# HGRN2 score products: two decay levels in one unbroken TensorE group, with a copy of the queries for the first level of a pair

## The chip, the core and the metric

The kernel runs on one core of a Trainium2 chip. The metric is the device time of one execution in microseconds (us), lower is better. TensorE is called PE below (its weight loads PEld), VectorE DVE, ScalarE ACT, GpSimd POOL, and SP is the engine that issues most DMAs.

## What is computed

One block of a diffusion transformer on 2048 tokens of width 1024 with 256 context tokens: a mixer of four HGRN2 heads and four retention heads, both run forwards and backwards, an output projection, and a gated convolutional FFN of width 2816. The change is in the HGRN2 heads. Their recurrence has a decay per token and per channel, so the scores of a chunk are not a plain product of queries and keys:

```python
def step(s, inp):
    qc, kc, vc, lfc = inp
    b = jnp.cumsum(lfc, axis=2)
    diff = b[:, :, :, None, :] - b[:, :, None, :, :]
    decay = jnp.where(mask[:, :, None], jnp.exp(jnp.minimum(diff, 0.0)), 0.0)
    attn = jnp.einsum('bhtsk,bhsk->bhts', qc[:, :, :, None, :] * decay, kc)
    o = (jnp.einsum('bhtk,bhkv->bhtv', qc * jnp.exp(b), s)
         + jnp.einsum('bhts,bhsv->bhtv', attn, vc))
```

`q`, `k` and the decay `f` are 128 channels wide; `v` has 128 columns. The score of tokens t and s needs the product of all decays between them.

## The kernel before

The program has three parts: a prologue (modulation vectors, the first norm, the first weights), the eight mixer heads, and the output projection with the FFN. The dense products run in float16 with three products per pair of blocks (`mm3`, lines 98 to 103) on blocks combined in a seven-product scheme.

A head is worked in four steps of 512 tokens, so the HGRN2 heads have 16 steps. A step has two threads of code, which `weave` (line 1003) deals out alternately: the sweep of this step (`hg_sweep1`, line 871) and the projections of the next one (`hg_proj`, line 843, mostly float16 products named `pa`, `pb`, `pc`, `p`). A scheduler then puts each engine's instructions into one fixed order by what is ready and by priority, which is the order in which the code was written unless a piece is marked as urgent. On the chip every engine works through its own fixed order and waits at an instruction whose inputs are not there.

`hg_sweep1` computes the scores of a chunk of 128 tokens by levels 1, 2, 4, ..., 64. At level `lv` a block of `2*lv` tokens is cut into halves; keys `K` and queries `Q` carry the decay up to the border between the halves, for both directions at once. After each level DVE multiplies half of `K` and of `Q` by the decay of the other half (lines 906 and 911), which extends them to the next level. So the products of a level must have read `K` and `Q` before these two multiplications, and the next level's products come after them.

- The diagonal (`sd`, line 881) and the levels 1 to 16 (`sc`, line 895) each take 16 float32 products of 32 by 32 outputs, one for each block of 32 tokens; level 32 (`sf`, line 902) takes 16 of that size and level 64 takes 8 of 64 by 64. A float32 product shows as two passes in the trace, so a level of 16 products is 32 records of PE. They use 32 (or 64) columns of the array, one column group after another.
- For levels 1 to 16 ACT first copies the wanted halves of `K` into a packed tile `Kl` (line 891); `Q` is read where it lies, with a stride.
- The result of a level lies in one of two PSUM buffers with the tag `sc`. DVE merges it into the tile `Ad` under a mask (line 913); the diagonal goes to `Ad` by a copy on ACT (line 882); levels 32 and 64 are copied by ACT into the full score tile `A` (lines 916 and 919).
- Then come transposes of `K` (`kp`), state increments (`uf`, `ub`) and the output products (`op`), all of them float32 products of 128 columns.

ACT and DVE also move the results of the projections out of PSUM (for example `ct` by line 604, `V` by line 644, `FG` by line 782), from three PSUM buffers with the tag `pj`. ACT squares and splits the weights of the next head as well, which arrive by DMA as `raw` (line 742).

Of the kernel before, what the change touches and what calls it, by code (L numbers as in the profile page):

```python
# [9 lines left out]
F32 = mybir.dt.float32  # L10
# [8 lines left out]
P = 128  # L19
# [3 lines left out]
G = 512  # L23
# [6 lines left out]
NIN = 4608  # L30
EPS = 1e-6
WR = 2
KL = 3
B = 32
LEVELS = (1, 2, 4, 8, 16, 32, 64)

V_N1, V_N2, V_LB, V_HN, V_RN, V_BM = 0, 8, 16, 32, 36, 40
NV = 88
KEPT = ("K0", "K1", "Q0", "Q1", "FG", "KTt", "ou0")
BANKS = dict(pj=3, sc=2, tu=3)  # L40
BUFS = dict(z=14, vg=7, q=4, wr=2, xs=3, Kl=KL, A=2, gate=NG + 1)
H = G // 2
# [8 lines left out]
def view(t, off, dims):  # L51
    return bass.AP(t.tensor, t.offset + off, [t.ap[0]] + dims)


class Kern:
# [90 lines left out]
    def setup(self):  # L146
# [37 lines left out]
        mp = self.mp  # L184
        sc = mp.tile([2 * KT, P], F32, tag="Kl", bufs=KL, name="s_c")
        q = nc.gpsimd
# [4 lines left out]
        self.mod_loads()  # L191
        s2 = mp.tile([NV, P], F32, tag="Kl", bufs=KL, name="s2")
        for v, n, src in ((V_BM, 48, I["b_mod"].rearrange("o (a p) -> (o a) p", p=P)),
# [5 lines left out]
            q.dma_start(s2[v:v + n], src)  # L199
        s1 = mp.tile([4 * NF, P], F32, tag="Kl", bufs=KL, name="s1")  # L200
        q.dma_start(s1[:3 * NF], I["conv_w"].rearrange("o j (a p) -> (o j a) p", p=P))
# [13 lines left out]
    def small_vectors(self):  # L215
# [8 lines left out]

        mf = self.mp.tile([P, 5 * B], F32, tag="Kl", bufs=KL, name="mf")
        nc.gpsimd.dma_start(mf, self.I["masks"])
# [22 lines left out]
    def mod_rows(self, rows, nr, j4):  # L249
# [3 lines left out]
        if nr == 2:  # L253
            rs = self.mp.tile([P, 512], F32, tag="Kl", bufs=KL, name="modrow")
            if j4:
# [538 lines left out]
    def hg_context(self, pool, h, W, st):  # L794
# [10 lines left out]
        yield from self.single(*self.tm(w, self.hc, P), dq, lambda half: V[:, half:half + 1])  # L805
        Tc = pool.tile([P, 2, 2], F32, tag="T128", bufs=2, name="cT128")
        o = 2 * n
        for lv in LEVELS:
            nb = n // (2 * lv)
# [61 lines left out]
    def hg_sweep1(self, pool, h, g, slot, pr, st):  # L871

        nc = self.nc
        FG, K, Q, qs, ks, V, gate = (pr[n] for n in ("FG", "K", "Q", "qs", "ks", "V", "gate"))

        A = pool.tile([P, 4, P], F32, tag="A", bufs=2, name="A")
        Ad = pool.tile([P, 4, B], F32, tag="Ad", bufs=1, name="Ad")
        blocks = [(c, slice(j, j + B), c * P + j) for c in range(4) for j in range(0, P, B)]
        sc = self.ps("sc", [P, 4, B], "sd")
        for c, js, o in blocks:  # L880
            nc.tensor.matmul(sc[js, c], ks[:, o:o + B], qs[:, o:o + B], start=True, stop=True, skip_group_check=True)
        nc.scalar.copy(Ad, sc)
        yield
        T = FG
        T128 = pool.tile([P, 2, 4], F32, tag=f"T128_{slot}", bufs=1, name="T128")
        for li, lv in enumerate(LEVELS):
            nb = G // (2 * lv)
            near = 2 * lv <= B
            if near:
                Kl = pool.tile([P, G], F32, tag="Kl", bufs=KL, name="Kl")  # L890
                nc.scalar.copy(Kl.rearrange("p (b two i) -> p b two i", two=2, i=lv), view(K, 0, [[2 * lv, nb], [G + lv, 2], [1, lv]]))
                sc = self.ps("sc", [P, 4, B], "sc")
                for c, js, o in blocks:
                    qv = view(Q, o, [[2 * lv, B // (2 * lv)], [G + lv, 2], [1, lv]])
                    nc.tensor.matmul(sc[js, c], Kl[:, o:o + B], qv, start=True, stop=True, skip_group_check=True)
            else:

                sc = self.ps("sc", [P, 4, lv], "sf")
                for c in range(4):
                    for j in range(P // lv):  # L900
                        o, q = c * P + j * lv, c * P + (j ^ 1) * lv
                        nc.tensor.matmul(sc[j * lv:(j + 1) * lv, c], K[:, j % 2, o:o + lv], Q[:, 1 - j % 2, q:q + lv],
                                         start=True, stop=True, skip_group_check=True)

            kv = view(K, 0, [[G + lv, 2], [2 * lv, nb], [1, lv]])
            nc.vector.tensor_tensor(kv, kv, view(T, 1, [[G // lv - 1, 2], [2, nb], [0, lv]]), ALU.mult)
            Tl = T
            T = self.totals(T, T128 if lv == 64 else
                            pool.tile([P, 2, nb], F32, tag="Ta" if lv in (1, 4, 16) else "Tb", bufs=1, name="T2"))
            qv = view(Q, 0, [[G + lv, 2], [2 * lv, nb], [1, lv]])  # L910
            nc.vector.tensor_tensor(qv, qv, view(Tl, G // lv + 1, [[-G // lv - 1, 2], [2, nb], [0, lv]]), ALU.mult)
            if near:
                nc.vector.copy_predicated(Ad, view(self.masks, li * B, [[0, 4], [1, B]]), sc)
            else:
                for j in range(P // lv):
                    nc.scalar.copy(A[j * lv:(j + 1) * lv, :, (j ^ 1) * lv:((j ^ 1) + 1) * lv], sc[j * lv:(j + 1) * lv])
                if lv == B:
                    for _, js, o in blocks[:P // B]:
                        nc.scalar.copy(A[js, :, o:o + B], Ad[js])
            yield  # L920

        KTt = self.slot_tile([P, 2, 4, P], F32, "KTt", "KTt")
        for d in range(2):
            kp = self.ps("tu", [P, 4, P], "kp")
            for c in range(4):
                nc.tensor.transpose(kp[:, c], K[:, d, c * P:(c + 1) * P], self.ident)
            nc.scalar.copy(KTt[:, d], kp)
        yield
        uf = self.ps("tu", [P, 4, P], "uf")
        for c in range(4):  # L930
            nc.tensor.matmul(uf[:, c], KTt[:, 0, c], V[:, c], start=True, stop=True, skip_group_check=True)
        ou, qf = self.slot_tiles(slot)
        Uf = ou[:, 1].rearrange("p (c t) -> p c t", t=P)
        nc.scalar.copy(Uf, uf)
        nc.scalar.copy(qf, Q[:, 1])
        ub = self.ps("tu", [P, 4, P], "ub")
        for c in range(4):
            nc.tensor.matmul(ub[:, c], KTt[:, 1, c], V[:, c], start=True, stop=True, skip_group_check=True)
        yield
        op = self.ps("sc", [P, 4, P], "op")  # L940
        Sb = st["Sb"]
        for i, c in enumerate((3, 2, 1, 0)):
            nc.tensor.matmul(op[:, c], A[:, c], V[:, c], start=(i == 0), stop=False, skip_group_check=True)
            nc.tensor.matmul(op[:, c], Q[:, 0, c * P:(c + 1) * P], Sb, start=False, stop=(i == 3), skip_group_check=True)
            S2 = KTt[:, 0, c] if c else pool.tile([P, P], F32, tag="S1", bufs=2, name="Sb")
            nc.vector.scalar_tensor_tensor(S2, Sb, T128[:, 1, c:c + 1], ub[:, c], ALU.mult, ALU.add)
            Sb = S2
            yield
        st["Sb"] = Sb
        opart = ou[:, 0].rearrange("p (c t) -> p c t", t=P)  # L950
        nc.scalar.copy(opart, op)
        st["grp"][g] = dict(qf=qf, Uf=Uf, T128=T128, op=opart, gate=gate)

# [4 lines left out]
    def fwd_state(self, pool, st, r, tag):  # L958
# [3 lines left out]
        for c in range(4):  # L962
            nc.tensor.matmul(o2[:, c], r["qf"][:, c * P:(c + 1) * P], Sf, start=True, stop=True, skip_group_check=True)
            S2 = r["Uf"][:, c] if c < 3 else pool.tile([P, P], F32, tag="S0", bufs=3, name="Sf")
            nc.vector.scalar_tensor_tensor(S2, Sf, r["T128"][:, 0, c:c + 1], r["Uf"][:, c], ALU.mult, ALU.add)
            Sf = S2
# [317 lines left out]
    def ret_sweep1(self, pool, h, g, slot, pr, st):  # L1284
# [31 lines left out]
        nc.vector.scalar_tensor_tensor(opart, ob, self.qd[:, 1, h:h + 1], opart, ALU.mult, ALU.add)  # L1316
        st["grp"][g] = dict(qf=qf, Uf=Uf, T128=view(self.cd, h, [[NH, 2], [0, 4]]), op=opart)

# [625 lines left out]
def _consts():  # L1944
    s = np.arange(P)
    masks = []
    for h in LEVELS:
        same = (s[:, None] // (2 * h)) == (s[None, :] // (2 * h))
# [49 lines left out]
```

## Time and profile before

| | us |
|---|---|
| three timed runs | 2592.52, 2597.32, 2599.94 (median 2597.32) |
| the profiled execution | 2600.73 |
| its span, first to last instruction | 2599.0 |
| prologue until the first score product | 0 to 84 |
| HGRN2 heads | 84 to 740 |
| retention heads, output projection, FFN | 740 to 2599 |

The profiled execution is 3.4 us (0.13%) above the median of the timed runs. A page of the profile gives the busy time of each engine and the chain of work that ended last. A matmul's record is longer than the time until the next one starts, since products overlap in the array, so what a stretch of products costs is read from starts, not from durations. In a timeline, neighbouring records of one kind are merged into one row with their count.

### The profile page before, as it was taken

How to read it: one execution, taken by the hardware profiler on the slowest of the kernel's cores; microseconds unless marked ns; L12 is line 12 of the kernel's file. 1: busy time of each engine (PE TensorE's matmuls, PEld its weight loads, DVE VectorE, ACT ScalarE, POOL GpSimd, SP SyncE). 2: the span in 40 equal slices, each digit the busy share in tenths (PEclk: the TensorE clock that was granted, in tenths of full speed). 3: DMA queues.
4: the chain of work that ended last, by engine and by line, in shares of the span. 5: the costliest groups of instructions: out<-in, count | busy, mean ns of one | idle time of the engine just before them, and what ended most of it. 6: DMA issues, size and time to landing. Idle time of an engine off the chain costs nothing.

```text
span 2599.0 us, 56245 instructions
## 1 busy us (share of the span) xinstructions
PE 2500.6 (96%) x22761; PEld 1647.9 (63%) x22761; DVE 1895.5 (73%) x4304; ACT 1351.0 (52%) x2879; POOL 385.4 (15%) x377
## 2 busy tenths in 40 slices
PE   5899998999999999999999999999999999999998
PEld 3788887889899999895544444444444444444443
DVE  6798586776878777785659777888888887223766
ACT  7886466564655454553647555556655554211221
POOL 1100000000000000001232343434443442000000
PEclk8999999999999999999999999999999999999999
DMA  8334342442558667794421332233233326544552
GB/s 308 113 135 132 119 147 83 139 152 67 180 164 284 214 214 253 246 332 148 167 82 48 124 112 99 101 111 114 102 106 110 122 90 246 197 173 154 211 213 83
DMA packets 144789, 402.36 MB, mean 155 GB/s; under 512 B 16144, under 2 KB 16372, under 8 KB 139921
## 3 DMA queue, kind: packets, MB, share of 16 engines
q1 hardware_dynamic: 134976, 381.81, 42.0%
q10 hardware_dynamic: 9248, 16.79, 2.0%
q8 instruction: 178, 2.92, 0.5%
q14 instruction: 83, 0.67, 0.1%
q0 software_dynamic: 304, 0.17, 0.0%
HBM read 302.77 MB, written 95.94 MB: 153 GB/s over the span
## 4 chain that ended last, share of the span: by engine, by line
PE 72%; DVE 11%; issue 6%; ACT 5%; DMA 5%; POOL 1%; SPq 0%; ACTq 0%; DVEq 0%; POOLq 0%
PE pa L101 8%; PE pa L102 8%; PE pa L103 8%; PE pd L102 5%; PE pd L101 5%; PE pd L103 5%; PE pc L101 3%; PE pc L103 3%; PE pc L102 3%; PE pb L101 2%; PE pb L102 2%; PE pb L103 2%; DMA raw<-in_w_in_dram 2%; PE opp L101 2%; PE opp L103 2%
## 5 line engine op out<-in xcount | busy, mean ns | idle before, releaser
L101 PE MATMUL pa<-feat,w 128*128 128x512 f16 x704 | 265.5, 382 | 7.2 <-DVE tb L638 4.1
L103 PE MATMUL pa<-feat,w 128*128 128x512 f16 x704 | 268.5, 382 | 1.3 <-DVE w L704 1.3
L102 PE MATMUL pa<-feat,w 128*128 128x512 f16 x704 | 268.4, 381 | 0.0
L102 PE MATMUL pd<-wd,actl 128*128 128x512 f16 x616 | 233.3, 379 | 0.0
L103 PE MATMUL pd<-wd,actl 128*128 128x512 f16 x616 | 233.3, 379 | 0.0
L101 PE MATMUL pd<-wd,actl 128*128 128x512 f16 x616 | 232.6, 379 | 0.0
L103 PEld LDWEIGHTS <-w 128*128 128x128 f16 x1232 | 120.8, 98 | 150.3 <-DVE w L704 4.3
L102 PEld LDWEIGHTS <-w 128*128 128x128 f16 x1232 | 120.8, 98 | 149.4 <-issue 10.9
L101 PEld LDWEIGHTS <-w 128*128 128x128 f16 x1232 | 120.8, 98 | 142.0 <-issue 3.1
L102 PEld LDWEIGHTS <-hx 128*128 128x128 f16 x1824 | 178.7, 98 | 6.3 <-issue 4.2
L101 PEld LDWEIGHTS <-hx 128*128 128x128 f16 x1824 | 179.0, 98 | 2.4 <-DVE qs L690 0.3
L103 PEld LDWEIGHTS <-hx 128*128 128x128 f16 x1824 | 178.8, 98 | 1.3 <-issue 0.4
L1474 POOL TENSOR_TENSOR ssq<-ssq 128x1 f32<-128x1 f32 x16 | 6.7, 417 | 1136.1 <-ACT junk L1469 1136.1
L1719 ACT ACTIVATE st<-act,modT 128x512 f16<-128x512 f32 x154 | 107.3, 717 | 113.0 <-DVE act L1709 61.5
L1720 DVE SCALAR_TENSOR_TENSOR st<-act,modT,st 128x512 f16<-128x512 f32 x154 | 143.9, 967 | 29.0 <-ACT st L1719 28.6
L101 PE MATMUL pa<-w_vg,hx 128*128 128x128 f16 x800 | 141.6, 219 | 2.0 <-ACT ct L604 1.2
L102 PE MATMUL pa<-w_vg,hx 128*128 128x128 f16 x800 | 141.6, 219 | 0.3 <-DVE w_vg L704 0.3
L103 PE MATMUL pa<-w_vg,hx 128*128 128x128 f16 x800 | 141.5, 219 | 0.0
L103 PE MATMUL pc<-feat,w 128*128 128x512 f16 x352 | 133.3, 379 | 2.0 <-DVE w L704 2.0
L101 PE MATMUL pc<-feat,w 128*128 128x512 f16 x352 | 133.4, 379 | 0.3 <-ACT tb L604 0.3
L102 PE MATMUL pc<-feat,w 128*128 128x512 f16 x352 | 133.4, 379 | 0.0
L704 DVE SCALAR_TENSOR_TENSOR w<-wur,p2s,w 128x512 f16<-128x512 f32 x132 | 122.8, 938 | 6.0 <-ACT w L703 6.0
(553 smaller groups left out, 7305.1 us busy)
## 6 DMA issues: line engine op xcount, KB each, us to landing
hx<-hxd SPq DMA_DIRECT2D x212, 512.0 KB, 5.2
actd<-st SPq DMA_DIRECT2D x154, 256.0 KB, 2.0
actl<-actd SPq DMA_DIRECT2D x28, 1024.0 KB, 5.2
wur<-in_w_up_dram SPq DMA_DIRECT2D x44, 512.0 KB, 3.6
raw<-in_w_in_dram SPq DMA_DIRECT2D x36, 512.0 KB, 4.6
wm<-in_w_mod_dram SPq DMA_DIRECT2D x64, 256.0 KB, 4.2
hxd<-hx SPq DMA_DIRECT2D x28, 512.0 KB, 4.1
wdb<-in_w_down_dram SPq DMA_DIRECT2D x44, 256.0 KB, 3.8
```

Of the source, the lines that this page charges most:

```text
L101: mm(ps, lhs(0), rhs(0), start=start, stop=False, skip_group_check=True)
L102: mm(ps, lhs(0), rhs(1), start=False, stop=False, skip_group_check=True)
L103: mm(ps, lhs(1), rhs(0), start=False, stop=stop, skip_group_check=True)
L704: nc.vector.scalar_tensor_tensor(W[m][:, 1], v, sc, W[m][:, 0], ALU.mult, ALU.subtract)
L1474: nc.gpsimd.tensor_tensor(ssq[:, 0:1], ssq[:, 0:1], ssq[:, 1:2], ALU.add)
L1719: nc.scalar.activation(p[:, 0], v, AF.Copy, scale=s)
L1720: nc.vector.scalar_tensor_tensor(p[:, 1], v, s, p[:, 0], ALU.mult, ALU.subtract)
```

## The change

1. The score products are collected instead of issued level by level. The diagonal and level 1 form one group, levels 2 and 4 the next, levels 8 and 16 the third; level 32 and level 64 stay groups of their own. So a step has five groups of 32, 32, 32, 16 and 8 products, where it had eight.
2. A pair of levels lies side by side in one PSUM buffer of the tag `sc`.
3. Levels 2 and 8 (`PAIRED`) come first in their pair. Their products are now issued after `Q` has already been multiplied for the next level, so ACT copies the wanted half of `Q` into a tile `Ql`, as it does with `K`. These are two new ACT copies a step, 32 in all. `Ql` shares the buffers of `Kl`, of which there are four now instead of three.
4. Within a group the later level's products come first; the first of them leads, and all others are ordered behind it. Groups are marked as high priority, those of levels 32 and 64 too, so that the scheduler puts them ahead of other work that is ready, with nothing between.
5. The copy of the diagonal into `Ad` and the masked merges come when a group is finished, the two merges of a pair one after the other.

The number of products, of DVE multiplications and of merges is the same.

```diff
-KL = 3
+KL = 4
+PAIRED = (2, 8)
...
-        sc = self.ps("sc", [P, 4, B], "sd")
-        for c, js, o in blocks:
-            nc.tensor.matmul(sc[js, c], ks[:, o:o + B], qs[:, o:o + B], start=True, stop=True, skip_group_check=True)
-        nc.scalar.copy(Ad, sc)
-        yield
+        half = lambda t, lv, o, n: view(t, o, [[2 * lv, n // (2 * lv)], [G + lv, 2], [1, lv]])
...
+        score, due = [(ks, lambda o: qs[:, o:o + B], None)], []
...
                 Kl = pool.tile([P, G], F32, tag="Kl", bufs=KL, name="Kl")
-                nc.scalar.copy(Kl.rearrange("p (b two i) -> p b two i", two=2, i=lv), view(K, 0, [[2 * lv, nb], [G + lv, 2], [1, lv]]))
-                sc = self.ps("sc", [P, 4, B], "sc")
-                for c, js, o in blocks:
-                    qv = view(Q, o, [[2 * lv, B // (2 * lv)], [G + lv, 2], [1, lv]])
-                    nc.tensor.matmul(sc[js, c], Kl[:, o:o + B], qv, start=True, stop=True, skip_group_check=True)
+                nc.scalar.copy(Kl.rearrange("p (b two i) -> p b two i", two=2, i=lv), half(K, lv, 0, G))
+                if lv in PAIRED:
+                    Ql = pool.tile([P, G], F32, tag="Kl", bufs=KL, name="Ql")
+                    nc.scalar.copy(Ql.rearrange("p (b two i) -> p b two i", two=2, i=lv), half(Q, lv, 0, G))
+                    score.append((Kl, lambda o, Ql=Ql: Ql[:, o:o + B], li))
+                else:
+                    score.append((Kl, lambda o, lv=lv: half(Q, lv, o, B), li))
+                    sc = self.ps("sc", [P, len(score), 4, B], "sc")
+                    lead = None
+                    with self.tc.high_priority():
+                        for n, (k, q, _) in reversed(list(enumerate(score))):
+                            for c, js, o in blocks:
+                                with self.tc.issue_after(lead.ins) if lead else nullcontext():
+                                    mm = nc.tensor.matmul(sc[js, n, c], k[:, o:o + B], q(o), start=True, stop=True, skip_group_check=True)
+                                lead = lead or mm
+                    due, score = [(sc[:, n], m) for n, (_, _, m) in enumerate(score)], []
...
+                with self.tc.high_priority():
...
+            if li == 0:
+                nc.scalar.copy(Ad, due.pop(0)[0])
+                yield
...
             if near:
-                nc.vector.copy_predicated(Ad, view(self.masks, li * B, [[0, 4], [1, B]]), sc)
+                for v, m in due:
+                    nc.vector.copy_predicated(Ad, view(self.masks, m * B, [[0, 4], [1, B]]), v)
+                due = []
```

The scheduler's order changes with this on the engines while the HGRN2 heads run; from a few instructions after the first retention products on, each engine's order is the same as before. On SP the rows are the same but for a few loads of `raw` and of norm rows, which stand one to four places earlier or later among the loads of `hx`; POOL's order is unchanged. Three places show how PE and ACT change.

PE at the second step of the third head, where the output products of the step before (`op`, `uf`, `ub`) meet the diagonal of this one (`sd`). Before:

```order
L943 MATMUL op<-V,A 128x128
L881 MATMUL sd<-qs,ks 32x32 x14
L931 MATMUL uf<-V,KTt 128x128 x4
L881 MATMUL sd<-qs,ks 32x32 x2
L101 LDWEIGHTS w_z
```

The same place now, where the first row of score products is level 1 and the second the diagonal:

```order
L958 MATMUL op<-V,A 128x128
L902 MATMUL sc<-Q,Kl 32x32 x16
L902 MATMUL sc<-qs,ks 32x32 x16
L941 MATMUL kp<-ident,K 128x128 x8
L959 MATMUL op<-cs_7555,Q 128x128
```

The diagonal was cut in two by `uf`; now it and level 1 stand as one piece of 32 products.

PE a little later in the same step. Before, level 1 (`o` are the forward products of the head before):

```order
L963 MATMUL o_7930<-ou,qf 128x128 x3
L895 MATMUL sc<-Q,Kl 32x32 x7
L944 MATMUL op<-KTt,Q 128x128
L943 MATMUL op<-V,A 128x128
L944 MATMUL op<-KTt,Q 128x128
L943 MATMUL op<-V,A 128x128
L944 MATMUL op<-KTt,Q 128x128
L895 MATMUL sc<-Q,Kl 32x32 x9
L102 LDWEIGHTS w_q
```

Now, levels 4 and 2, the group that follows the one shown above:

```order
L103 LDWEIGHTS w_q
L103 MATMUL pa<-hx,w_q 128x256
L902 MATMUL sc<-Q,Kl 32x32 x16
L902 MATMUL sc<-Ql,Kl 32x32 x16
L946 MATMUL uf<-V,KTt 128x128 x4
L953 MATMUL ub<-V,KTt 128x128 x4
```

Level 1 was cut by five products of the output; now 16 products from `Q` and 16 from the copy `Ql` run without a break. Counted over the whole program, the 1920 score products stand in 169 unbroken runs before (81 of them whole groups of 16) and in 80 runs now (48 of 32, 16 of 16, 16 of 8).

ACT at the first step of the third head, where the packed copies stand between evacuations of the projections (`ct`, `cb`, `gate`). Before:

```order
L891 COPY Kl<-K 128x512
L604 COPY ct<-pa 128x256
L604 COPY cb<-pc 128x256
L891 COPY Kl<-K 128x512 x2
L865 ACTIVATE gate<-cb,dq 128x256
```

Now:

```order
L605 COPY ct<-pa 128x256
L889 COPY Kl<-K 128x512
L892 COPY Ql<-Q 128x512
L605 COPY cb<-pc 128x256
L889 COPY Kl<-K 128x512
L866 ACTIVATE gate<-cb,dq 128x256
```

Between the two evacuations `ct` and `cb`, which stood next to each other, there are now a copy of `K` and one of `Q`.

More of the change, by code (lines that the diff above doesn't have):

```diff
@@ L896, in hg_sweep1 @@
             else:
                 sc = self.ps("sc", [P, 4, lv], "sf")
[L899 to L903, printed above, removed]
+                with self.tc.high_priority():
+                    for c in range(4):
+                        for j in range(P // lv):
+                            o, q = c * P + j * lv, c * P + (j ^ 1) * lv
+                            nc.tensor.matmul(sc[j * lv:(j + 1) * lv, c], K[:, j % 2, o:o + lv], Q[:, 1 - j % 2, q:q + lv],
+                                             start=True, stop=True, skip_group_check=True)
```

## The prediction

> **What bounds the kernel now.** I read the page first, then the busy times by stretch, then the chain of work that ended last within the stretch that the change touches.
>
> ```profile
> PE 2500.6 (96%) x22761; PEld 1647.9 (63%) x22761; DVE 1895.5 (73%) x4304; ACT 1351.0 (52%) x2879; POOL 385.4 (15%) x377
> ```
>
> ```profile
> core 0: us, PE busy (x) PEld busy (x) DVE busy (x) ACT busy (x) POOL busy (x), PEclk, DMA share, GB/s
> 0.00:84.00 84.00, 56.42 (x413) 37.61 (x414) 52.18 (x134) 63.45 (x123) 13.14 (x33) 0.86 0.67 257
> 84.00:740.00 656.00, 619.58 (x10230) 554.25 (x10228) 505.52 (x1357) 414.71 (x1010) 6.10 (x12) 0.99 0.39 129
> 740.00:2599.00 1859.00, 1824.58 (x12124) 1056.00 (x12122) 1337.85 (x2815) 872.84 (x1747) 366.16 (x332) 1.00 0.46 159
> ```
>
> PE is the busiest engine everywhere after the prologue. The columns behind the length of a stretch are the busy times of PE, PEld, DVE, ACT and POOL. In the HGRN2 stretch (84 to 740 us) PE is busy for 619.6 of 656 us (94%), DVE for 77% and ACT for 63%. So 36.4 us of that stretch are idle on PE, and a saving of PE time there has room to count. The two other stretches keep their order nearly whole, so I give them no change. The granted clock is 0.99, so there is nothing to win from it.
>
> ```profile
> by line: issue 12.7%; PE pa L101 7.8%; PE pa L102 7.6%; PE pa L103 7.5%; DMA raw<-in_w_in_dram 6.0%; PE sc L895 3.7%; PE pc L101 3.3%; PE pb L101 3.2%; PE pb L102 3.1%; PE pc L102 3.1%; PE pb L103 3.1%; PE pc L103 3.1%; PE uf L931 2.1%; PE
> ...
> 80.31 35.98 issue
> 119.91 34.48 issue
> ...
> 340.68 6.67 DMA raw<-in_w_in_dram
> ```
>
> This is the chain within the stretch, as shares of its 656 us. It is not PE alone: 6.0% is loads of head weights (`raw`), and two pieces of 36.0 and 34.5 us are "issue", where the chain finds no releaser. The level products of line 895 have 3.7%, or 24.3 us.
>
> ```profile
> L895 PE MATMUL sc<-Q,Kl 128*32 128x32 f32 x2560 | 44.0, 202 | 3.9 <-ACT Kl L891 2.8 <-DVE Q L911 1.1
> ...
> L902 PE MATMUL sf<-Q,K 128*64 128x64 f32 x256 | 11.3, 228 | 1.5 <-DVE Q L911 1.5
> ...
> L881 PE MATMUL sd<-qs,ks 128*32 128x32 f32 x512 | 10.9, 200 | 0.0
> ...
> L902 PE MATMUL sf<-Q,K 128*32 128x32 f32 x512 | 7.3, 199 | 0.9 <-DVE Q L911 0.9
> ```
>
> These are all score products: 73.5 us of records. Line 895 is busy for 44.0 us, so 24.3 / 44.0 = 55% of its time is on the chain. The last columns are idle time before them: 6.3 us in all, so the groups rarely wait for their inputs.
>
> **The change part by part.** First what an unbroken group costs. Records overlap, so I go by starts.
>
> ```profile
> 302.83 0.22 PE L101 MATMUL pa<-w_vg,hx 128*128 128x128 f16 x1
> 302.98 0.46 PE L895 MATMUL sc<-Q,Kl 128*32 128x32 f32 x32
> 303.37 0.23 PE L102 MATMUL pa<-w_vg,hx 128*128 128x128 f16 x1
> 303.44 0.22 PE L103 MATMUL pa<-w_vg,hx 128*128 128x128 f16 x1
> 303.49 0.22 PE L101 MATMUL pa<-w_vg,hx 128*128 128x128 f16 x1
> ```
>
> The float16 products start 0.055 us apart, so the next would have started at 302.89. It starts at 303.37: the group of 32 passes costs 0.48 us. It begins 0.09 us after 302.89, which is a cost of entering it. Now a group that is cut:
>
> ```profile
> 481.74 0.39 PE L944 MATMUL op<-cs,Q 128*128 128x128 f32 x2
> 481.96 0.39 PE L943 MATMUL op<-V,A 128*128 128x128 f32 x2
> 482.28 0.45 PE L881 MATMUL sd<-qs,ks 128*32 128x32 f32 x28
> 482.65 1.16 PE L931 MATMUL uf<-V,KTt 128*128 128x128 f32 x8
> 483.74 0.26 PE L881 MATMUL sd<-qs,ks 128*32 128x32 f32 x4
> 483.93 0.28 PE L101 MATMUL pa<-hx,w_z 128*128 128x256 f16 x1
> ```
>
> Two float32 passes of 128 columns take 0.22 us from start to start, so `uf` could have started at 482.18; it starts at 482.65, and the 28 passes cost 0.47 us. The 4 passes take 0.19 us to the next start, and with the entry of 0.09 they cost 0.28. Together 0.75 us against 0.48 uncut: **a cut costs 0.27 us**. From the 4 to the 28 passes the time to the next start grows by 0.37 - 0.19 = 0.18, or 0.0075 us a pass. So the passes are cheap and the change of shape is dear.
>
> Joining two whole groups: 64 passes cost 0.48 + 32 x 0.0075 = 0.72 us, against 2 x 0.48 = 0.96. That saves 0.24; the pattern of 32 passes in 0.39 us to the next start would give 32 x 0.39/32 = 0.39 for the second half and a saving of 0.09. I take 0.22, near the row of the passes, and keep 0.09 as the low end.
>
> By the order of the built programs the score products form 169 unbroken runs before and 80 after. The 16 steps have 8 groups each, 128, so 169 - 128 = 41 cuts go, and 48 pairs are joined:
>
> - 41 cuts x 0.27 = 11.1 us
> - 48 joins x 0.22 = 10.6 us (4.3 at the low end)
> - **sum: 21.6 us of PE time**, 15.4 at the low end.
>
> The entry and exit gaps are what a rule of the Trainium skill speaks of: "TensorEngine Tiling (Array Packing)", section Key Properties, says that changing the tiling mode, though not the tile, drains TensorE; the rows agree, since passes of 32 columns follow each other cheaply and cost only where they meet 128 columns. "TensorE: Matmul & The Clock Gate", section Single matmul latency, gives 398 cycles at 2.4 GHz beyond the streaming, 0.166 us; an estimate from it is 89 fewer runs x 0.166 = 14.8 us with one drain a run, and 29.5 with two, on both sides of the sum above.
>
> Next, how much of it shortens the time. At least the share of the score products that is on the chain, 55%: 0.55 x 21.6 = 11.9 us. At most all of it, since PE is busy for 94% of the stretch. The two rows point to different ends, and part of the chain (70 us of "issue") is not known, so I take the middle: **16.8 us**.
>
> What is added: 32 copies `Ql`. The copy of `K` is the same size.
>
> ```profile
> L891 ACT COPY Kl<-K 128x512 f32<-128x512 f32 x80 | 54.2, 678 | 18.3 <-PE sc L895 13.3 <-DVE K L906 4.6
> ...
> L911 DVE TENSOR_TENSOR Q<-Q,T 128x512 f32<-128x512 f32 x96 | 66.0, 687 | 8.2 <-PE sc L895 7.9
> ...
> L604 ACT COPY ct<-pa 128x256 f32<-128x256 f32 x40 | 14.8, 369 | 17.5 <-PE pa L103 17.4
> ```
>
> 32 x 0.678 = 21.7 us on ACT, which goes from 414.7 to 436.4 busy us of 656 (67%). They lie beside PE's projections, and I cost them at 0; the bounds are 0 and 21.7 us, if each delays PE by its length. Queued behind them on ACT are the evacuations `ct` and `cb`, for whose PSUM buffers the projections wait. That is rival two.
>
> The path of the levels within a step: before, two levels cost twice (0.48 group + 0.69 multiplication of `Q`) = 2.34 us. After, it is the copy `Ql` 0.68, the multiplication 0.69, the later level's half of the group, some 0.37, and again 0.69 = 2.43. With 32 pairs that is 2.9 us, if it were the chain everywhere; I take 0, since the multiplication no longer waits for PE (7.9 us of such waits above). The diagonal is not a level, and its join is free on this path. Merges, DVE work and products stay the same in number, at 0. The loads of `raw` that move by a few places on SP have 6.0% of the chain but take the same time; I take 0; one load more or less on the chain, 6.7 us by the row above, is the outer bound either way.
>
> Sum against the profiled execution: 2600.7 (span 2599.0 and 1.7 around it) - 16.8 = 2583.9. The median of the runs is 3.4 lower, so the forecast is 2597.3 - 16.8 = **2580.5 us**.
>
> **The rivals.**
>
> One, the whole saving and more: all 21.6 us count, and the 6.3 us of waits before score groups go too. 2597.3 - 27.9 = 2569.4. For it: the multiplication of `Q` in a first level no longer waits for PE. Against it: 45% of the score time is off the chain, and other waits stay.
>
> Two, no change that can be told: the copies `Ql` delay the evacuations. For it is this row:
>
> ```profile
> 510.99 0.27 PE L101 MATMUL pc<-hx,w_z 128*128 128x256 f16 x1 [2.36 <-ACT V L644]
> ```
>
> Here PE waited 2.36 us for an evacuation that ACT had not reached. The gain falls below 7.8 us, 0.3% of the time (about what a measurement can tell from no change), once the 32 copies cost 9.0 us together, 0.28 us each. With half of each exposed: 16.8 - 10.9 = 5.9 us gain, 2591.4 us. Against it: ACT itself is idle for 37% of the stretch, and it waits for PE far more (17.5 us before `ct` alone) than PE for it.
>
> Three, slower: the lead of a pair waits at the head of PE's queue. A group that is put first and kept whole can't be filled with other work when its input is late; all projections behind it wait too, and with them ACT and DVE.
>
> ```profile
> 95.11 0.54 PE L895 MATMUL sc<-Q,Kl 128*32 128x32 f32 x32 [0.90 <-ACT Kl L891]
> ```
>
> Such a wait was 0.90 us here. The place is the lead of levels 4 and 16, which needs two multiplications of `Q` and two copies since the last group: 32 x 0.90 = 28.8 us, a net loss of 12.0, 2609.3 us. It decides from 16.8/32 = 0.53 us a lead; over 0.3% slower from 0.77. Against it:
>
> ```profile
> 300.86 0.70 DVE L911 TENSOR_TENSOR Q<-Q,T 128x512 f32<-128x512 f32 x1
> ...
> 303.52 0.69 DVE L911 TENSOR_TENSOR Q<-Q,T 128x512 f32<-128x512 f32 x1 [0.51 <-PE sc L895]
> ```
>
> ```profile
> 305.43 0.46 PE L895 MATMUL sc<-Q,Kl 128*32 128x32 f32 x32
> ```
>
> `Q` was ready at 301.56 and the group came at 302.98; then 304.21 and 305.43. So the fixed order lets a group come 1.2 to 1.4 us after its input even where levels follow each other closely. If that margin stays, leads don't wait.
>
> **How the numbers follow.** The forecast, with 11.9 to 21.6 us gained (2575.7 to 2585.4): 0.60. Rival one: 0.11. Rival two: 0.17. Rival three: 0.12. So faster by over 0.3% (below 2589.5) has 0.71, within 0.3% 0.17, slower 0.12. The range goes from 2566, beyond rival one by half of the join's uncertainty of 6.3 us, to 2598, which takes in the half-exposed copies and most of rival two. Left out are rival three and the tails, some 0.19.
>
> **What would show it.** The score products should come in 80 runs; a run of 64 passes should take 0.6 to 0.7 us to the next start, and each step should lose some 1 us of PE work. The first retention product should come some 17 us earlier, with the rest of the kernel as long as before. `Ql` should cost 0.6 to 0.7 us each. Rival two shows as longer waits of `pa`, `pb`, `pc` for ACT; rival three as idle time before the score products far above 6.3 us. The forecast is wrong if that idle time grows by more than 10 us, or if the waits of the projections for ACT do; and the step "the middle of 55% and all" is wrong if PE's score time falls by 21 us and PE's idle time in the stretch grows by as much.

## The result, and the profile after

| | before | after |
|---|---|---|
| median of 4 runs each, us | 2597.74 | 2574.81 |
| lowest and highest, us | 2592.52, 2599.94 | 2573.06, 2576.89 |
| ratio of the medians | | 0.9915, 95% interval 0.9903 to 0.9926 |
| the profiled execution, us (span) | 2600.73 (2599.0) | 2573.06 (2571.0) |

The kernel is 22.9 us (0.9%) faster. The forecast was 16.8 us faster, 2580.5 us; the measured time lies 5.7 us below it, between the forecast and rival one, and 0.9 us past the fast end (2575.7) of the band that the forecast's 0.60 was given for. The two profiled executions lie 27.7 us apart, since that of before is 3.0 us above its median and that of after is the fastest of its four, so what the traces show below adds up to more than 22.9.

First the busy times of the whole span in the page after, then the stretches of the trace after (length, then busy PE, PEld, DVE, ACT, POOL, granted clock, DMA share, GB/s).

```profile
PE 2476.4 (96%) x22761; PEld 1640.7 (64%) x22761; DVE 1897.2 (74%) x4304; ACT 1362.0 (53%) x2907; POOL 385.0 (15%) x377
```

```profile
0.00:84.00 84.00, 55.99 (x448) 38.25 (x449) 53.81 (x138) 65.20 (x127) 13.10 (x33) 0.86 0.67 259
84.00:740.00 656.00, 621.77 (x10534) 571.38 (x10532) 524.54 (x1404) 437.48 (x1069) 6.47 (x12) 0.99 0.40 134
740.00:2571.00 1831.00, 1798.69 (x11785) 1031.06 (x11783) 1318.82 (x2764) 859.35 (x1713) 365.46 (x332) 1.00 0.45 160
```

PE is busy 24.2 us less in the whole span. A fixed window of 84 to 740 us now holds work of the next stretch, so the cut that compares is the first retention product (`rsc`): its line in the answers on that tile, of before and of after (durations, then first and last start):

```profile
L1290 PE MATMUL rsc<-K x128: 275/275/328, 738.7 to 1150.9; 128*128 128x128 f32 x128
```

```profile
L1305 PE MATMUL rsc<-K x128: 275/275/328, 712.3 to 1125.1; 128*128 128x128 f32 x128
```

It starts 26.4 us earlier. The rest of the span is as long as before (2599.0 - 738.7 = 1860.3, and 2571.0 - 712.3 = 1858.7), so the gain is made in the HGRN2 stretch. The windows from 84 us to that product, of before and of after:

```profile
84.00:738.70 654.70, 618.28 (x10219) 552.95 (x10217) 505.14 (x1356) 414.09 (x1009) 6.10 (x12) 0.99 0.39 130
```

```profile
84.00:712.30 628.30, 594.07 (x10184) 544.08 (x10182) 505.78 (x1352) 424.15 (x1034) 6.47 (x12) 0.99 0.40 135
```

PE's busy time falls by 24.2 us. Its idle time falls by 2.2, from 36.4 to 34.2. So in this pair the saving of PE time was not given back as waits. By the count of starts in the table below, 19.9 us of the fall belong to the score products; the other 4.3 us are no more than the 4.6 us by which two executions of the changed kernel differ outside score and idle time. Now one joined group of levels 2 and 4 in the timeline of after:

```profile
312.88 0.27 PE L102 MATMUL pa<-hx,w_q 128*128 128x256 f16 x1
312.99 0.27 PE L103 MATMUL pa<-hx,w_q 128*128 128x256 f16 x1
313.19 0.46 PE L902 MATMUL sc<-Q,Kl 128*32 128x32 f32 x32
313.46 0.49 PE L902 MATMUL sc<-Ql,Kl 128*32 128x32 f32 x32
313.88 0.94 PE L946 MATMUL uf<-V,KTt 128*128 128x128 f32 x6
```

From the usual next start, 312.99 + 0.11 = 313.10, the 64 passes cost 0.78 us, and 0.69 from their own start. The groups that touch the sum and the waits, from the answers by line of after:

```profile
L902 PE MATMUL sc<-Q,Kl 128*32 128x32 f32 x1536 | 23.3, 204 | 2.2 <-ACT ou L966 1.1 <-ACT Kl L889 0.9 <-DVE Q L924 0.2
L912 PE MATMUL sf<-Q,K 128*32 128x32 f32 (+1 forms) x768 | 18.5, 209 | 0.3 <-issue 0.3
L902 PE MATMUL sc<-Ql,Kl 128*32 128x32 f32 x1024 | 15.7, 199 | 0.0
L902 PE MATMUL sc<-qs,ks 128*32 128x32 f32 x512 | 7.8, 199 | 0.0
...
L892 ACT COPY Ql<-Q 128x512 f32<-128x512 f32 x32 | 20.7, 645 | 11.1 <-DVE Q L924 6.7 <-DVE rs_y L90 3.6 <-DVE rs_t L88 0.6
```

PE's idle time before score products is 2.5 us where it was 6.3, and a `Ql` copy takes 0.645 us.

### The profile page after: what moved, and what is told of

It reads as the page before. It is cut to its first block, busy times and chain, and to the rows that moved or that the text cites. A ratio compares the mean times of both kernels' runs of the same rounds, so it can differ in the third digit from the quotient of the medians.

```text
span 2571.0 us, 56272 instructions
## 1 busy us (share of the span) xinstructions
PE 2476.4 (96%) x22761; PEld 1640.7 (64%) x22761; DVE 1897.2 (74%) x4304; ACT 1362.0 (53%) x2907; POOL 385.0 (15%) x377
## 3 DMA queue, kind: packets, MB, share of 16 engines
q8 instruction: 178, 2.92, 0.5%
## 4 chain that ended last, share of the span: by engine, by line
PE 74%; DVE 10%; issue 6%; ACT 4%; DMA 4%; POOL 1%; SPq 0%; DVEq 0%; ACTq 0%; POOLq 0%
PE pa L102 8%; PE pa L103 8%; PE pa L104 8%; PE pd L104 5%; PE pd L102 5%; PE pd L103 5%; PE pc L102 4%; PE pc L104 4%; PE pc L103 4%; PE pb L102 3%; PE pb L104 3%; PE pb L103 3%; PE opp L102 2%; PE opp L104 2%; PE opp L103 2%
## 5 line engine op out<-in xcount | busy, mean ns | idle before, releaser
L102 PE MATMUL pa<-hx,w_z 128*128 128x256 f16 x464 | 126.5, 273 | 6.2 <-ACT ct L605 5.9
```

The lines of the kernel that those rows point to most:

```text
L102: mm(ps, lhs(0), rhs(0), start=start, stop=False, skip_group_check=True)
```

## The experiments

All ratios are against the kernel before, run beside each, whose median was 2597.7 to 2599.9 us. "Score" is the time that the score products cost PE, summed over the unbroken runs: from the start of the product ahead of a run to the start of the product behind it, less the usual spacing of the product ahead, less idle time. "Idle" is PE's idle time from 84 us to the first retention product. Both come from the one profiled execution.

| kernel | runs of score products | score, us | idle, us | median, us | ratio (95%) |
|---|---|---|---|---|---|
| before | 169 | 79.1 | 36.4 | 2597.7 | |
| the change | 80 | 59.2 | 34.2 | 2574.8 | 0.9915 (0.9903-0.9926) |
| after_again | 80 | 59.3 | 33.3 | 2575.6 | 0.9913 (0.9900-0.9927) |
| pairs_loose | 124 | 70.0 | 34.7 | 2593.2 | 0.9980 (0.9971-0.9989) |
| single_whole | 127 | 67.5 | 34.0 | 2589.3 | 0.9966 (0.9954-0.9979) |
| copies_twice | 79 | 59.0 | 32.6 | 2578.4 | 0.9921 (0.9906-0.9936) |
| four_groups | 64 | 55.7 | 35.9 | 2574.4 | 0.9910 (0.9897-0.9924) |
| products_twice | 80 | 89.2 | 70.6 | 2655.6 | 1.0214 (1.0197-1.0231) |
| buffers_only | 166 | 78.1 | 26.0 | 2586.7 | 0.9959 (0.9947-0.9972) |
| pool_copies | 79 | 59.0 | 26.7 | 2571.0 | 0.9897 (0.9884-0.9911) |
| single_whole_four | 127 | 68.3 | 30.2 | 2583.6 | 0.9941 (0.9929-0.9954) |
| own_buffer | 81 | 58.8 | 28.0 | 2566.2 | 0.9881 (0.9865-0.9897) |
| four_groups_pool | 63 | 55.4 | 39.7 | 2581.1 | 0.9933 (0.9921-0.9944) |
| own_buffer_pool | 79 | 59.7 | 37.7 | 2582.2 | 0.9936 (0.9922-0.9949) |

**after_again**: the changed kernel once more, to have it beside the others.

> The changed kernel once more, as the measure for the runs beside it. All theories: 2574.8 us, within 3 us.

2575.6 us, 23.1 under before. Score and idle come out within 1 us of the first profile, but the span is 3.8 us longer (2574.8 against 2571.0): all the rest took 2482.2 us here and 2477.6 there.

**pairs_loose**: pairs and `Ql` copies, but no priority and no order behind a lead.

```diff
-                    with self.tc.high_priority():
+                    with nullcontext():
...
-                                with self.tc.issue_after(lead.ins) if lead else nullcontext():
+                                with nullcontext():
...
-                with self.tc.high_priority():
+                with nullcontext():
```

> The pairs of levels and the copies of the queries stay; the high priority of the groups and the order within a group are taken out, so other work may cut them. The built order has 124 unbroken runs of score products (169 before the change, 80 with it). Theory one, the number of unbroken runs sets the gain, about 0.24 us a run: 45 runs fewer than before, 11 us gained, 2587 us. Theory two, the gain comes from putting the groups first in the order: nearly all of it gone, 2595 us or more. Theory three, the gain comes from the copy of the queries, which frees the multiplication of Q from its wait for the products: nearly all of it stays, 2577 us or less.

Only 5.5 us faster, between theory one (2587) and theory two (2595), nearer the second; theory three (2577) is out. The score products lose 9.1 us though they are still cut, but the other float32 products of 128 columns between 84 us and the first retention product (`kp`, `op`, `uf`, `ub`, `tp`, `o` and some smaller ones) cost 4.7 us more from start to start (114.4 us, against 109.7 before and 109.7 in the whole change). Why they do was not looked into further.

**single_whole**: the eight groups of a step, each kept whole and urgent, without pairs, `Ql` or the fourth buffer.

```diff
-KL = 4
+KL = 3
...
-PAIRED = (2, 8)
+PAIRED = ()
...
+        with self.tc.high_priority():
+            for c, js, o in blocks:
+                with self.tc.issue_after(lead.ins) if lead else nullcontext():
+                    mm = nc.tensor.matmul(sd[js, c], ks[:, o:o + B], qs[:, o:o + B], start=True, stop=True, skip_group_check=True)
+                lead = lead or mm
```

> Eight groups a step as before the change, each level by itself and no copy of the queries, but every group up to level 16 at high priority behind a lead, and levels 32 and 64 at high priority. 127 unbroken runs. Theory one: 42 runs fewer than before, at 0.27 us each for a cut, 11 us gained, 2586 us. Theory two (priority): nearly the whole gain, 2578 us or less. Theory three (the copy of the queries): no gain, 2595 us or more.

9.3 us faster, nearest to theory one (2586). 42 runs fewer take 11.6 us of score time, 0.28 us a cut, as the prediction priced it (0.27). Here too the float32 products of 128 columns cost more, by 4.2 us (113.9). From here to the whole change the score time falls by another 8.3 us for 47 joins: 0.18 us a join, where 0.22 was taken.

**copies_twice**: each `Ql` copy is made twice.

```diff
                     nc.scalar.copy(Ql.rearrange("p (b two i) -> p b two i", two=2, i=lv), half(Q, lv, 0, G))
+                    nc.scalar.copy(Ql.rearrange("p (b two i) -> p b two i", two=2, i=lv), half(Q, lv, 0, G))
```

> The changed kernel with every copy of the queries made twice into the same tile, so 32 more ACT copies of 0.68 us, 21.7 us of ACT in all; 79 unbroken runs. If ACT's copies lie beside other work, as the forecast had it: 2575 us, within 3 us of the changed kernel. If they delay the evacuations or the leads: up to 21.7 us more, 2585 to 2597 us.

2.8 us slower than after_again, with overlapping intervals; idle is 32.6 us against 33.3. ACT has some 21 us more to do and PE does not wait longer for it. The intervals leave room for a price of up to some 8 us.

**four_groups**: the diagonal with levels 1 and 2, then 4 with 8, then 16 with 32, and 64 alone.

```diff
-PAIRED = (2, 8)
+PAIRED = (1, 4, 16)
...
```

The part left out lets the group of level 32 take in level 16, with its lead, and moves the copy of the diagonal and the merges behind the longer groups.

> Four groups a step instead of five: the diagonal with levels 1 and 2, levels 4 and 8, levels 16 and 32, level 64; three copies of the queries a step instead of two. 64 unbroken runs instead of 80. If the number of runs sets the time, at 0.18 us a join as measured in the changed kernel: 16 x 0.18 = 2.9 us and some 1 us for level 1 read from a packed copy, 2571.5 us. If the longer leads (a copy of Q more before levels 2 and 32) make PE wait: 2580 us or more, with more than 8 us of idle time before score products.

The score time falls by 3.5 us more, near what the count of joins had it, but the time is that of the change within the interval (2571.5 was expected), and PE's idle time before score products is 5.2 us instead of 2.5.

**products_twice**: the products of the three groups up to level 16 are issued twice.

```diff
-                        for n, (k, q, _) in reversed(list(enumerate(score))):
+                        for n, (k, q, _) in 2 * list(reversed(list(enumerate(score)))):
```

> The changed kernel with the products of the three groups up to level 16 issued twice in their group, with the same result: 48 groups of 128 passes instead of 64, about 30 us more of PE time by the starts in the changed kernel's trace (32 x 0.61 + 16 x 0.69). Theory one, PE time in this stretch counts in full: 2606 us. Theory two, only the share of the score products that lies on the chain counts, 55%: 2592 us. The forecast's middle: 2599 us.

The score time grows by 30 us, as priced, but the kernel by 80 against the change. Idle grows by 36 us, and most of it has no releaser. The waits of PE from 84 to 795 us, longest sums first (total, times, longest), and a place in the timeline inside a group:

```profile
PE sc L902 <- issue: 23.3, 11, 5.5
PE pa L102 <- issue: 6.0, 4, 4.0
PE op L958 <- ACT A L931: 4.5, 2, 3.7
PE pc L104 <- issue: 4.1, 2, 2.4
```

```profile
414.38 0.36 PE L902 MATMUL sc<-Ql,Kl 128*32 128x32 f32 x19
417.16 0.32 PE L902 MATMUL sc<-Ql,Kl 128*32 128x32 f32 x12 [2.42 <-issue]
417.41 0.23 PE L102 MATMUL pc<-w_vg,hx 128*128 128x128 f16 x1
```

PE stops for 2.42 us in the middle of a group whose inputs it has already read. So this kernel can't price PE time, and the question it was made for, whether all of it counts or only the share on the chain, stays without an experiment of its own; what it shows is told at the end.

**buffers_only**: the kernel before with `KL = 4` in place of 3, nothing else.

> The kernel before with four buffers for the packed copies instead of three and nothing else; 166 unbroken runs. All theories: no change, 2598 us within 3 us. If the buffer was what held the levels back: 2590 us or less.

11.6 us faster, where I had expected next to nothing. The score time is unchanged (78.1); the gain is idle time, 10.4 us of it:

```profile
84.00:724.00 640.00, 614.03 (x10223) 552.00 (x10222) 507.16 (x1357) 411.95 (x1008) 5.75 (x12) 0.99 0.40 133
```

So either the fourth buffer is half of the gain of the change, or it happens to give another order with fewer waits. The two later kernels that touch the buffers, single_whole_four and own_buffer, bear on this.

**pool_copies**: the change with `Ql` copied by GpSimd.

```diff
-                    nc.scalar.copy(Ql.rearrange("p (b two i) -> p b two i", two=2, i=lv), half(Q, lv, 0, G))
+                    nc.gpsimd.tensor_copy(Ql.rearrange("p (b two i) -> p b two i", two=2, i=lv), half(Q, lv, 0, G))
```

> The changed kernel with the copies of the queries on GpSimd instead of ACT. ACT loses 21.7 us of work; the copies reach the group later if GpSimd is slower. If ACT's copies cost something: 2572 us or less. If they lie beside other work and GpSimd is in time: 2575 us. If the lead then waits, as in the rival that a late lead holds up PE: 0.5 us in each of 32 groups would give 2591 us.

4.6 us under after_again, idle 26.7 us. That is what the expectation gave as the sign that ACT's copies cost something (2572 us or less); the two kernels further down that also copy on GpSimd don't bear it out. Its copies take longer than on ACT:

```profile
L892 POOL COPY Ql<-Q 128x512 f32<-128x512 f32 x32 | 25.9, 809 | 551.2 <-DVE Q L924 222.4 <-PE cup L828 201.5 <-DVE rs_t L89 56.1
```

**single_whole_four**: single_whole with `KL = 4`.

> The eight groups of a step kept whole and urgent, not joined, no copies of the queries (as in single_whole, -9.3 us), and the fourth buffer of the tag Kl (as in buffers_only, -11.6 us). Theory 'two savings that add': the buffer takes idle time, the whole groups take PE time, so about -21 us, near 2577, with PE's score time about 68 us and PE's idle time between 84 us and the first retention product about 26. Then the joins with their copies are worth only some 2 us net. Theory 'one gain, reached in two ways': the buffer frees the same PE time or the same waits that the whole groups free, so about -10 to -13, near 2587, and the joins are worth the other 10. Bounds 2574 to 2592.

14.6 us faster: neither the 21 of a plain sum nor 10 to 13. The buffer is worth 5.2 us here, not 11.6. The score time, 68.3 us, is that of single_whole.

**own_buffer**: the whole change, but `Ql` has one buffer of its own and `Kl` three, as before.

```diff
-KL = 4
+KL = 3
...
-                    Ql = pool.tile([P, G], F32, tag="Kl", bufs=KL, name="Ql")
+                    Ql = pool.tile([P, G], F32, tag="Ql", bufs=1, name="Ql")
```

> The whole change, but the copies Ql have a buffer of their own, and Kl has three as before; the memory is the same in sum. Theory 'the fourth buffer counts as a freer rotation of Kl': the copies of Kl wait for PE's last group again, PE's idle time rises by up to 10 us from 34, about 2580 to 2585. Theory 'with pairs the rotation is not what limits': within 2 us of the whole change, near 2575, because a step needs as many Kl and one Ql at a time.

2566.2 us, 32.0 us under before and the fastest of all; neither theory had that. (Its score and idle time come from an execution of 2573.5 us; the other three took 2565.4 to 2566.5. How much of these 7 us is idle time isn't shown.) A freer rotation of `Kl` is thus not where the gain of the change comes from. ACT waits 15.1 us for PE before `Kl`, the first releaser in its row, more than the 13.3 us of before, and the kernel is faster:

```profile
L889 ACT COPY Kl<-K 128x512 f32<-128x512 f32 x80 | 54.4, 679 | 27.3 <-PE sc L902 15.1 <-DVE K L919 6.4 <-DVE K L853 3.2
```

**four_groups_pool**: four groups with `Ql` on GpSimd.

> Four groups a step (64 unbroken runs) with the three copies Ql a step on GpSimd in place of ScalarE. In five groups that move was worth 3.8 us (pool_copies against the whole change). Theory 'the copies stand in ScalarE's queue ahead of what PE waits for': 3 copies a step in place of 2, so about 1.5 times as much, 5 to 6 us off four_groups, near 2569 and the fastest so far; idle 30 us or less. Theory 'the path of a step is what limits four groups': the GpSimd copies are longer, so no gain over four_groups or a loss, 2573 to 2580, with more idle time before score products than the 5.2 us of four_groups.

6.7 us slower than four_groups, so the second theory held in kind (a loss, and more idle time before score products), 1 us above its 2573 to 2580. The idle time is 39.7 us, 7.5 of it before score products.

**own_buffer_pool**: own_buffer with `Ql` on GpSimd.

> The whole change with a buffer of its own for Ql (own_buffer was 9.5 us under the whole change beside the kernel before) and with the Ql copies on GpSimd (pool_copies was 3.8 under it). Theory 'each relief has a price of its own': they add, about 4 us under own_buffer, near 2562, with PE's idle time from 84 us to the first retention product about 22. Theory 'the idle time left is a matter of how the rows of a program happen to fall': PE's score time stays 59, the idle time comes out anywhere in the 26 to 40 us that the ten kernels so far showed, so 2565 to 2580 and most likely above own_buffer.

Of two edits that each gained 4 to 9 us on the change, both together are 16 us slower than own_buffer and some 5 to 7 slower than the change. The score time stays at 59.7, the idle time goes from 28.0 to 37.7 us. The second theory held in kind: the idle time lies in its 26 to 40 us, the time 2 us above its 2580. Each copy takes 1.025 us here, where it took 0.809 in pool_copies; why was not looked into:

```profile
L892 POOL COPY Ql<-Q 128x512 f32<-128x512 f32 x32 | 32.8, 1025 | 574.4 <-DVE Q L924 460.0 <-DVE rs_t L89 51.7 <-DVE Sb L961 26.2
```

**What the table says together.** In every kernel but products_twice the profiled span is the sum of score and idle plus 2478 to 2488 us (before 2599.0 - 115.5 = 2483.5; the change 2571.0 - 93.4 = 2477.6; pairs_loose, the highest, 2592.3 - 104.7 = 2487.6). So two numbers describe all of them to within 10 us. The score time follows the number of runs. The idle time does not follow the score time: the five-group kernels (the change, after_again, copies_twice, own_buffer, pool_copies, own_buffer_pool) have 26.7 to 37.7 us, 32.1 in the mean; the kernels without joins (before, buffers_only, single_whole, single_whole_four) 26.0 to 36.4, 31.7 in the mean.

Averaged over kernels of one score time, which mixes several orders, before and buffers_only have 78.6 us of score time and 2592.2 us, and the five-group kernels (the change and after_again taken as one) 59.2 us and 2574.6 us: 17.6 us of time for 19.4 us of score time. Single pairs scatter widely around that. From buffers_only to the change, which both have four buffers, 18.9 us of score time give 11.9 us, and idle time grows by 8.2; from buffers_only to single_whole_four, 9.8 give some 3 to 5; from before to own_buffer, 20.3 give 32.0; and pairs_loose, with 8.1 us less score time than buffers_only, is 6.5 us slower than it.

Some of the scatter goes with the granted clock. Over the 44 executions of the kernel before that ran beside the experiments, 0.001 less of mean granted clock (it lay between 0.987 and 0.992) went with 1.6 us more. The runs of single_whole had 0.9874 in the mean where the kernel before had 0.9894 beside it, and those of buffers_only 0.9904 against 0.9891; by that slope some 3 us of the one and 2 us of the other are the clock's.

Where idle time comes from in one order and not in another can be seen at its largest single piece before, in the timelines of PE and of ACT before:

```profile
444.68 0.26 PE L101 MATMUL pa<-w_vg,hc 128*128 128x128 f16 x1 [4.34 <-ACT cFG L782]
```

```profile
438.67 1.28 ACT L782 ACT_TABLE_LOAD   x1
439.96 0.40 ACT L782 ACTIVATE cFG<-cb,dq 128x128 f32<-128x128 f32 x1
...
440.67 1.28 ACT L1185 ACT_TABLE_LOAD   x1
441.97 0.69 ACT L1185 ACTIVATE re<-ramp,tmp 128x128 f32<-128x128 f32 x2
442.68 1.28 ACT L782 ACT_TABLE_LOAD   x1
443.97 0.40 ACT L782 ACTIVATE cFG<-ct,dq 128x128 f32<-128x128 f32 x1
```

The scheduler put a set-up activation of the retention heads (line 1185) between two of line 782. Going from line 782 to line 1185 and back loads a table for 1.28 us each time, and PE waits for the row behind. The Trainium skill, "ScalarE: Activation LUTs", section What ACT_TABLE_LOAD costs, gives the same 1283 ns and a drain of about 1380 ns with it; the next row here starts 0.01 us after the load's end, so this trace shows the load without the drain. From 84 to 740 us ACT has 9 such loads before and 5 after, 5.1 us less of ACT time. Nothing in the change speaks of them; that they move because all rows move is argued. They don't sort the kernels either: own_buffer has 5 loads up to the first retention product and 28.0 us of idle time, own_buffer_pool 6 and 37.7, single_whole_four 9 and 30.2. In after the largest sum of PE's waits is another one, again with ACT:

```profile
PE pa L102 <- ACT ct L605: 6.9, 6, 3.0
```

## Why the prediction was right, and which term was too small

- **PE as the bound of the stretch**: right. Its busy time is what moved, and the span behind the stretch kept its length.
- **Runs and their prices**: right in kind, 8% too high in size. The runs are 80. 21.6 us of PE time were forecast, 19.9 measured (79.1 - 59.2). A cut costs 0.28 us in single_whole against 0.27; a join saves 0.18 us and not 0.22. The Trainium skill ("TensorEngine Tiling (Array Packing)", section Key Properties) says that a change of tiling mode drains TensorE. Between the prediction's two estimates for that, 14.8 us with one drain a run and 29.5 with two, the 19.9 us lie about a third of the way up. The term that was mis-sized is the join. The prediction let the second half of a joined group cost 32 x 0.0075 = 0.24 us; by the same count of starts a group of two later levels costs some 0.79 us against 0.48 for one level, so the second half costs 0.30 and the join saves 0.18. A group of the diagonal and level 1 costs some 0.86, and its join saves only 0.10. From their own start the 32 groups of later levels take 0.69 us, within the 0.6 to 0.7 named, and the 16 with the diagonal 0.78, above it.
- **The share that counts, "the middle of 55% and all"**: this step took 4.8 us off, and the runs don't bear out its reason. It read the chain's share of line 895 as the least that a saving is worth and the whole as the most. Single pairs of kernels lie on both sides of that: 3 to 5 us for 9.8 from buffers_only to single_whole_four, 32.0 for 20.3 from before to own_buffer. In the pair of the change idle time on PE did not grow by a part of the saving but fell by 2.2 us; with all of the 19.9 us counted, 3.0 of the 22.9 us are left. The mean over the orders, 17.6 us for 19.4, is near all of it, with a scatter that doesn't exclude the forecast's 78%. That the products behind a shorter group move up whether the chain passes through the group or not, in a stretch where PE is busy for 94%, fits this but was only argued. "All of it" as the likeliest would have given 2597.3 - 21.6 = 2575.7.
- **The fourth buffer**: the sum had no term for it, and it belonged in the bounds. By itself it gives 11.6 us (buffers_only), on single_whole 5.2; the whole change without it in the rotation gains 9 us more (own_buffer), not less. So it has no price that could be added. At equal buffers, from buffers_only, the change gains 11.9 us and not 22.9, so how much of the gain came with the buffer depends on the pair that is taken. That the difference is a matter of which order results was argued from these signs; it was not tried with a neutral edit of the order.
- **`Ql` at nothing**: not contradicted. A second set of copies costs 2.8 us, which the intervals don't tell from nothing, and shows in no longer wait; the upper bound of 21.7 us was far off. Taking the copies off ACT gained 4.6 us in pool_copies and lost 6.7 and 16 in the two other kernels, so their own price is hidden in what each order does to the waits. Rival two did not occur: the waits of `pa`, `pb` and `pc` for ACT make about 12 us before and 11 after.
- **Rival three, the lead at the head of the queue**: did not occur. Idle time before score products is 2.5 us for all 80 runs, the largest piece 1.1 us. It is 5.2 us in four_groups and 7.5 in four_groups_pool. That larger groups leave less room for their inputs to come early was only argued; single_whole_four, with the smallest groups, has 5.6.
- **Rival one**: its reason was right in part (waits before score groups fall from 6.3 to 2.5 us), its sum too large, since the PE term itself was too large by 1.7 us and idle time as a whole fell by only 2.2.

So the direction and the mechanism held: fewer places where shapes meet, less PE time, and in the mean over the orders nearly all of it in the time. The gain was missed by 6.1 us (22.9 for 16.8), and the term for PE time (1.7 us too high) and the share (4.8 us off) erred in opposite ways. That the range of 2566 to 2598 held the result owes something to its width. Kernels of one score time (2566.2, 2571.0, 2575, 2578.4 and 2582.2 us) spread over 16 us, against the 22.9 that were to be predicted, and no sum over the parts holds that spread.

## What to carry to other kernels

Price a regrouping of small products on a busy TensorE by the count of places where shapes meet (here 0.28 us for a cut, 0.18 for a join), and, where the engine is busy for nearly all of the stretch (94% here), take the whole of it as the middle of the forecast; here that was nearer to the mean over several orders than a discount by the chain of waits, though single pairs gave anything from a loss to half as much again. Where a scheduler makes the order, add a spread of its own for idle time that any edit reshuffles, here some 10 us between kernels of equal score time, and don't read two gains of such edits as a sum. The best version found here gives the copied queries their own buffer: 2566.2 us, a ratio of 0.9881 (0.9865 to 0.9897) to the kernel before.

## What the runs showed of the hardware that was not expected

- **A stop of PE inside long groups of tiny products.** With 128 passes in a group, PE stopped for up to 5.5 us where the profile shows nothing that it waited for; in the same view of the change the waits of score products on "issue" were 0.3 us. The pages of the two kernels show what differs in the queue that carries instructions (packets, MB), the change first:

```profile
q8 instruction: 178, 2.92, 0.5%
```

```profile
q8 instruction: 202, 3.31, 0.5%
```

A packet is 2.92 MB / 178 = 16.4 KB. The second kernel has 62432 instructions against 56272, 6160 more for 24 packets more: 257 instructions a packet, 64 bytes each. A group of 128 passes with their weight loads is 256 instructions, a packet's worth in about 1 us. That the stops are PE waiting for instructions fits these numbers, but it was only argued. The granted clock in the HGRN2 stretch was lower too:

```profile
84.00:795.20 711.20, 640.63 (x13281) 584.65 (x13280) 513.57 (x1355) 431.42 (x1037) 7.22 (x12) 0.97 0.36 120
```

- **The same copy on GpSimd takes 0.809 or 1.025 us in the mean**, in pool_copies and own_buffer_pool, against 0.645 on ACT in the change.
- **Level 64 is the dearest group for its size.** In the timeline of after its 16 passes of 64 columns stand between products that start 0.11 us apart:

```profile
237.00 0.27 PE L104 MATMUL pc<-hx,w_z 128*128 128x256 f16 x1
237.21 0.69 PE L912 MATMUL sf<-Q,K 128*64 128x64 f32 x16
237.82 0.28 PE L102 MATMUL pa<-hx,w_z 128*128 128x256 f16 x1
```

They cost 237.82 - 237.11 = 0.71 us (237.00 + 0.11 = 237.11 is the usual next start), nearly as much as the 64 passes of 32 columns above (0.78), with a quarter of the passes. What makes them dear was not tried.
